# First two experts' remainders on VectorE instead of GpSimd, and the last token tile's modulation on VectorE behind its choice of experts

## The chip, the cores and the metric

The kernel runs on one core of a Trainium2 chip, as one launch. The metric is the device time of the launch in microseconds; the median of three runs of the kernel before is 1519.3 us.

## The reference

The reference is a two-layer block over 512 latent and 256 context tokens of 1024 features. Each layer computes a modulated norm, an input projection, three mixers (attention, a state space scan, a Hyena convolution), an output projection with a gated residual, a second modulated norm and a mixture of 16 experts, of which a router picks two for each token. The part that matters here:

```python
        xl = xl + gt1[:, None, :] * mix_l
        ...
        hl2 = modulate(rmsnorm(xl, g_ffn[i]), sh2, sc2)
        ...
            xl = xl + gt2[:, None, :] * grouped_moe(hl2, w_router, router_bias, w_gate[i], w_up[i], w_down[i])

def grouped_moe(h, w_router, router_bias, w_gate, w_up, w_down):
    scores = jax.nn.sigmoid((t @ w_router).astype(jnp.float32))
    ...
    for e in range(N_EXPERTS):
        y = (jax.nn.silu(t @ w_gate[e]) * (t @ w_up[e])) @ w_down[e]
        out = out + combine[:, e:e + 1] * y
```

The first layer routes all 768 tokens, the second only the 512 latent ones.

## The kernel before

**Precision.** A weight or activation that enters a matmul is split in two: a rounded copy (fp32r, made by ScalarE, L209) and the remainder, the difference between the value and its copy (a subtraction, L210). Three matmuls (L222 to L224: copy by copy, copy by remainder, remainder by copy) stand for one product. The subtraction runs on VectorE, or on GpSimd where the caller of `split_in` gives `lo_eng`.

**Output projection and routing** (`out_proj`, L971 to L1073). It goes over tiles of 128 tokens: six in layer 0, four in layer 1. `first(t)` multiplies and adds the gated residual, writes the new stream to DRAM (`xd`, by the queue of SyncE), takes the row norm and modulates: `h2 = x * rs * A2 + B2`, written to `hd` in DRAM, from which the experts gather their rows. For all tiles but the last, VectorE does the product (L1029) and GpSimd the sum (L1030). For the last tile ScalarE scales (L1026) and GpSimd does both the product with A2 (L1027) and the sum (L1030), each over 128 x 1024 numbers. `second(t)` makes the router's logits (its weights hold the modulation already, so it reads the unmodulated tile), and after the last tile of a group (0-1, 2-3 and 4-5 in layer 0; 0-2 and 3 in layer 1) `choose` (L1116) picks each token's two experts: about 40 small operations of VectorE, one behind the other, with a sigmoid of ScalarE at the head (kept as `R.scored`) and some small matmuls in between. Its end is the table of each expert's tokens (L1205, L1206). `order` and `places` (L1215, L1238) sort the experts; the cast at L1246 is kept as `mark`.

**Experts** (`experts`, L1478). An expert's weights come in six pieces of 512 KB by SyncE's queue into a ring of raw buffers (5 in layer 0, 8 in layer 1), are copied (L209) into a ring of 12 or 10, and their remainders follow (L210); a raw buffer is free again when both are done. Pieces 0 to 3 serve the first product, 4 and 5 the second. `NPE[l][n]` says how many of the six remainders of the n-th expert of a layer are made on GpSimd, for the first two experts: 3 and 3 in layer 0, 5 and 3 in layer 1. All later experts have 2 of 6 there. For each tile of an expert the rows are gathered from `hd` (L1374, a DMA that GpSimd issues), transposed by TensorE (L1389), copied (L1395) and their remainder made on VectorE (`xl`, L1396); the products follow, with the gated product at L1425 (`g`) and its copy and remainder (`gl`, L1445) between the two.

**What sets the order.** The tile framework's scheduler puts every engine's instructions in an order by a simulated timeline when the program is built; where several are ready in it, the earlier one of the program goes first, and an engine that would be idle there takes a later one. On the chip each engine then works in that fixed order. `tc.issue_after(ins)` queues a block's instructions of `ins`'s own engine behind `ins`. The first experts' splits stand under it: in layer 0 both behind `mark` (an instruction of VectorE), in layer 1 the first behind `R.scored` (of ScalarE) and the second behind `mark`. So the first expert's VectorE remainders in layer 1 are held back only by their copies, and GpSimd's are not held back by either.

```python
early = mark is not None and n < len(NPE[l])
gen = expert_weights(l, e, wp, NPE[l][n] if early else 2, ...)
...
with tc.issue_after((mark if n >= NI[l] else R.scored).ins) if early else ExitStack():
    w = list(gen) if early else [next(gen)]
```

Of the kernel before, what the change touches and what calls it, by code (L numbers as in the profile page):

```python
# [14 lines left out]
AF = mybir.ActivationFunctionType  # L15
# [16 lines left out]
# feature-major blocks of the input projection: 6 hyena, 5 ssd conv, 3 gate  # L32
# [6 lines left out]
# columns of the constant array  # L39
# [15 lines left out]
# columns of the per-feature vectors: c, c_ctx, then per layer  # L55
# [4 lines left out]
# rows that every partition holds  # L60
# [25 lines left out]
# places of the experts: the first or last few stay where they are, the others come in the order of their tokens;  # L86
# that many of the first places have a second tile
NS = (1, 3)
LAST = (False, True)
KD = (6, 2)  # L90
# rows of each place's first tile, and of the second
# [4 lines left out]
NPE = (3, 3), (5, 3)  # L96
# [9 lines left out]
# the most rows of a light expert  # L106
LIGHT = 64, 0
# tiles of tokens that choose their experts together: the first, how many
# [7 lines left out]
def limits(l):  # L116
    """above how many tokens a place's last tile is left to a further one"""
    big = 1e9
    return [(P + CAP2[l][q] if CAP2[l][q] < P else big) if q < KD[l] else CAP[l][q] if CAP[l][q] < P else big
            for q in range(NE)]  # L120
# [3 lines left out]
def most_further(l):  # L124
    """the most further tiles that any counts of tokens ask for; all places but the NS that stay in falling order"""
# [16 lines left out]
def tile_kernel(tc, I, out, dbg=None):  # L142
# [10 lines left out]
    def banks(cfg):  # L153
        """shares the banks out among the chains that run side by side: kinds, number of banks; 0: of the first two"""
        if rings.get("cfg") == cfg:
            return
        if "end" in rings:
            rings["end"]()
        g = tc.tile_pool(name="psum", bufs=1, space=bass.MemoryType.PSUM, reuse_waits="tile")
        rings.update(cfg=cfg, pool=g.__enter__(), end=lambda: g.__exit__(None, None, None))  # L160
# [51 lines left out]
    def split_in(pool, nm, n, src, raws, his, lo_eng=None, raw_pool=None, raw_tag=None, parts=None):  # L212
        """a load in two parts"""
# [13 lines left out]
    # zeros around the two columns: a window of 32 has them where a block wants its rows  # L227
# [8 lines left out]
    def adaln_end():  # L236
        """the sums over the four groups of rows that the blocks of features have, by features"""
# [7 lines left out]
    def adaln(l, ch, wp, mb, j, n, step, wp2=None):  # L245
        """a block of 128 features; n of them, step apart, share a bank; it is the j-th of these"""
# [65 lines left out]
    def filters(pool):  # L312
# [11 lines left out]
        for l in range(DEPTH):  # L324
# [18 lines left out]
            # sum and difference of the two directions  # L343
# [13 lines left out]
            for c in cs:  # L357
# [6 lines left out]
                for o in range(2):  # L364
                    SD = pool.tile([P, 4, 2, 256], F32, name="SD", bufs=2)
                    for i in range(2 * n):
# [9 lines left out]
                        if i == 0:  # L376
                            # lag 0: the second direction has none, the first takes the bias
# [35 lines left out]
    def to_features(l, v, xn, pool, hh, hl, ks=range(8)):  # L413
        """normalised rows of a group of tokens: modulated, by features, in two parts"""
# [16 lines left out]
    def norm1(pool, wp, hh, hl):  # L431
        """the first norm, each block of features as soon as its modulation is there"""
        xt = [pool.tile([P, D], F32, name=f"xt{t}") for t in range(TA)]
        ss = sm.tile([P, TA], F32, name="ss0", bufs=1)
        for t in range(TA):
            SP.dma_start(xt[t], I["xin"][t * P:(t + 1) * P])
            # the squares themselves are not needed: they go where the last features will be
# [47 lines left out]
    def hy_proj(l, wp, hh, hl, pool, u, filler):  # L485
        """v split by parity of the token, x1 likewise, x2 by features"""
# [316 lines left out]
    def kv_weights(l, wp, places, lo_eng=None):  # L803
        """places: of the two parts, where not in the ring"""
# [26 lines left out]
    def rotate(l, qr, pool):  # L831
        """norm and rotation of queries and keys, where they are"""
        rl = l * RL_N
        # rotary tables with the gains of the norm
# [50 lines left out]
    def to_heads(l, qr, pool, QT, KT):  # L885
        """queries and keys by features, in two parts"""
# [84 lines left out]
    def out_proj(l, wp, wr, mix, pool, choose):  # L971
# [8 lines left out]
        def gates(v):  # L980
# [4 lines left out]
            # the router behind the modulation: its weights take the scale, the shift becomes a row  # L985
# [21 lines left out]
        def first(t, mh, ml, xt):  # L1007
# [17 lines left out]
            if t == nt - 1:  # L1025
                ACT.activation(h2, xt, AF.Copy, scale=rs)  # L1026
                POOL.tensor_mul(h2, h2, A2)  # L1027
            else:
                DVE.scalar_tensor_tensor(h2, xt, rs, A2, OP.mult, OP.mult)  # L1029
            POOL.tensor_add(h2, h2, B2)  # L1030
            SP.dma_start(hd[s], h2)
            yield xt, rs
# [27 lines left out]
        for t in range(nt):  # L1060
# [8 lines left out]
            nxt = next(g)  # L1069
            if last is not None and t < nt - IL:  # L1070
                second(t - 1, *last)
            last = nxt
        second(nt - 1, *last)  # L1073

    class Route:
        """each token's two experts, their slots and weights; tokens and weights of each tile, the expert of each place"""

        def __init__(self, l, nt, pool):
            self.l, self.nt, self.pool, self.H, self.NS = l, nt, pool, nt, NS[l]
            # those that stay, and those that are sorted  # L1080
# [19 lines left out]
        def tile(self, m, sh, nm):  # L1100
            """for m tiles of tokens, with the place for the most of them"""
# [3 lines left out]
        def first_max(self, x, m, n, rev, op, out):  # L1105
            """one-hot of the first of the largest, or what is left of it"""
# [9 lines left out]
        def choose(self, t0, m, lg):  # L1116
            """for m tiles of tokens from the t0-th"""
# [24 lines left out]
            # place of the token among those of its expert  # L1142
# [10 lines left out]
            # token and weight  # L1153
# [25 lines left out]
            # token and weight of each expert's n-th token  # L1179
# [21 lines left out]
            else:  # L1201
                if t1 == nt:
                    # of those that stay
# [4 lines left out]
        def pick(self, dst, v, n):  # L1208
            """of each place, what its expert has"""
# [5 lines left out]
        def order(self):  # L1215
            pool, pos, b0, sr = self.pool, self.pos, self.b0, self.sr
            nr = NE - self.NS
            # those that stay keep theirs, the others come in the order of their counts
# [19 lines left out]
        def places(self):  # L1238
# [10 lines left out]
            # light experts have sets of features one below the other  # L1249
# [8 lines left out]
        def where(self, i):  # L1258
            """of a tile: the expert that stays, or none, and the column of the tile"""
# [19 lines left out]
        def slots(self):  # L1279
            """rows of each token's two experts, the experts of the further tiles and the number of those"""  # L1280
            pool, nt, K, pos = self.pool, self.nt, KD[self.l], self.pos
            self.nov = nov = most_further(self.l)
            # the experts with more tokens than the tiles of their places hold
# [30 lines left out]
            # slots: tile of the place, second tile of the place, further tile  # L1314
# [11 lines left out]
            # expert of further tile o: the number of experts whose further tiles end at or before o  # L1326
# [11 lines left out]
        def further(self):  # L1338
            """tokens and weights of the further tiles"""
            pool, H, nov = self.pool, self.H, self.nov  # L1340
            # the further tile that each 128 tokens of each expert have; those with a place have none
# [18 lines left out]
    def expert_weights(l, e, wp, n_pool, tag, bufs, light):  # L1360
        """in six parts, each when it is asked for"""
# [16 lines left out]
    def groups(c):  # L1378
        """a light expert's few tokens: their sets of features that lie side by side on the array"""
        return 4 if c == 32 else 2  # L1380
# [24 lines left out]
    def expert_up(st, k0, k1, pool):  # L1405
# [11 lines left out]
        if xl is None:  # L1417
            # the first half of the groups is the gate, the other what it acts on
# [9 lines left out]
    def expert_mid(st, g, pool):  # L1428
# [3 lines left out]
        if light and groups(c) == 4:  # L1432
            # both halves of the features at once
# [44 lines left out]
    def experts(l, jobs, R, gate, wp, pool, mark=None):  # L1478
        """jobs: the tiles of an expert with their rows, and the expert"""
# [29 lines left out]
    def combine(l, order, si, xt, gate, pool, hh=None, hl=None):  # L1509
        """gate: of the two groups of tokens, or the gain of the last norm second"""  # L1510
# [31 lines left out]
    def weave(*gens, stop=None):  # L1542
        """steps of each in turn, at its rate; what they yield, if anything"""
# [15 lines left out]
    for l in range(DEPTH):  # L1559
# [26 lines left out]
        if l == 0:  # L1586
            wp, close_wp = opened("win", 2, side="right")
            kp, close_kp = opened("kv", side="right")
            # the first half lies where the results of the attention will be
# [382 lines left out]
```

## Time and profile before

| | us |
|---|---|
| median of 3 runs | 1519.3 |
| lowest and highest | 1517.98, 1522.31 |
| span of the profiled execution, first to last instruction | 1512.0 |
| own time of the profiled execution | not given; the median stands 7.3 above its span |
| TensorE, VectorE, ScalarE, GpSimd busy | 1270.4, 957.4, 656.3, 563.7 |

Spans are read from the first instruction. The work around the change lies at 540 to 680 (layer 0) and 1220 to 1320 (layer 1); the experts' stages go on to about 853 and 1481. In a row of a timeline stand the start, the duration, the engine, the line of the code, the operation, what is written and read, and in brackets how long the engine was idle before it and what ended that. A "q" behind an engine's name is its queue.

### The profile page before, as it was taken

To read this page: it belongs to the slowest core of one execution; us is meant where nothing else is said; L and a number is where in the kernel's file an instruction comes from. 1 tells how busy PE (TensorE), PEld (TensorE's weight loads), DVE (VectorE), ACT (ScalarE), POOL (GpSimd) and SP (SyncE) were. 2 spreads that over 40 slices of the span, in tenths; PEclk is the share of its full clock that TensorE was granted. 3 is DMA by queue.
4 is the path that set the end of the run, shared out by engine and by line. 5 is a ranking of instruction groups with operands and counts; after the bars stand their busy time and mean duration, and the time that the engine had idled before them with its cause. 6 is when DMAs were issued, how large, how long until landed. Compare 5 with 4: busy or idle time off the path is not lost. (4 is left out here: it accounts for less than half of the span.)

```text
span 1512.0 us, 24116 instructions
## 1 busy us (share of the span) xinstructions
PE 1270.4 (84%) x8787; PEld 964.7 (64%) x8787; DVE 957.4 (63%) x1824; ACT 656.3 (43%) x1244; POOL 563.7 (37%) x496
## 2 busy tenths in 40 slices
PE   5999999899799799669999539989898892699991
PEld 3787877677577587547656228867676782576540
DVE  6754732734767865893544384844597748877974
ACT  5331324445333542333544363544545624366662
POOL 3120311444343523262323360410486244544653
PEclk9999999997899999769999859999998996699996
DMA  8745976345555252178999851111311453688984
GB/s 297 244 147 175 294 231 228 97 143 181 185 159 171 101 198 98 56 240 313 341 327 333 287 214 57 57 56 43 133 50 43 156 210 119 236 297 296 358 314 177
DMA packets 102775, 289.67 MB, mean 192 GB/s; under 512 B 11421, under 2 KB 24109, under 8 KB 102000
## 3 DMA queue, kind: packets, MB, share of 16 engines
q1 hardware_dynamic: 89632, 243.92, 47.1%
q0 software_dynamic: 8480, 30.81, 5.9%
q10 hardware_dynamic: 4528, 13.24, 2.4%
q8 instruction: 73, 1.20, 0.3%
q14 instruction: 62, 0.51, 0.1%
HBM read 241.98 MB, written 45.95 MB: 190 GB/s over the span
## 5 line engine op out<-in xcount | busy, mean ns | idle before, releaser
L209 ACT CAST he<-re 128x1024 fp32r<-128x1024 f32 x150 | 153.0, 1048 | 74.7 <-DMA re<-in_we_dram 27.8
L210 POOL TENSOR_TENSOR le<-re,he 128x1024 fp32r<-128x1024 f32 x56 | 141.3, 2538 | 97.3 <-ACT he L209 74.6
L222 PE MATMUL bank<-hh,hw 128*128 128x512 f32 (+1 forms) x440 | 160.5, 365 | 3.2 <-ACT hw L209 3.2
L223 PE MATMUL bank<-hl,hw 128*128 128x512 f32 (+1 forms) x440 | 157.9, 359 | 0.0
L224 PE MATMUL bank<-hh,lw 128*128 128x512 f32 (+1 forms) x440 | 156.3, 356 | 0.4 <-DVE lw L210 0.4
L210 DVE TENSOR_TENSOR le<-re,he 128x1024 fp32r<-128x1024 f32 x94 | 138.2, 1494 | 22.7 <-ACT he L209 22.7
L222 PE MATMUL bank<-he,xh 128*128 128x512 f32 (+3 forms) x264 | 107.7, 408 | 2.1 <-DVE g L1425 2.0
L224 PE MATMUL bank<-he,xl 128*128 128x512 f32 (+3 forms) x264 | 105.7, 402 | 2.6 <-DVE xl L1396 2.6
L223 PE MATMUL bank<-le,xh 128*128 128x512 f32 (+3 forms) x264 | 106.3, 403 | 0.8 <-DVE le L210 0.8
L933 POOL TENSOR_SCALAR pt<-pt,su 128x768 f32<-128x768 f32 (+1 forms) x60 | 55.8, 934 | 115.4 <-DVE su L932 112.0
L1374 POOL DMA_INDIRECT xg<-hd,tk x40 | 43.9, 1096 | 140.1 <-PE bank L1389 53.1
L222 PEld LDWEIGHTS bank<-hh,hw 128*128 128x128 f32 x440 | 85.7, 195 | 15.6 <-ACT hw L209 3.3
L223 PEld LDWEIGHTS bank<-hl,hw 128*128 128x128 f32 x440 | 85.6, 194 | 12.0 <-issue 1.2
L224 PEld LDWEIGHTS bank<-hh,lw 128*128 128x128 f32 x440 | 84.6, 192 | 12.4 <-DVE lw L210 0.9
L259 PE MATMUL bank<-mraw,c 128*32 128x128 f32 x1536 | 70.4, 295 | 15.7 <-DMA mraw<-in_wm_dram 11.8
L210 DVE TENSOR_TENSOR lw<-rw,hw 128x1024 fp32r<-128x1024 f32 x34 | 41.7, 1228 | 55.3 <-ACT hw L209 52.6
L948 PE MATMUL bank<-ph,vt 128*64 128x128 f32 x624 | 54.7, 296 | 16.7 <-DVE ph L945 7.3
L209 ACT CAST hw<-rw 128x1024 fp32r<-128x1024 f32 (+1 forms) x36 | 37.7, 1049 | 70.8 <-PE bank L223 39.8
L259 PEld LDWEIGHTS bank<-mraw,c 128*32 128x32 f32 x1536 | 40.0, 114 | 40.1 <-DMA mraw<-in_wm_dram 16.5
L223 PE MATMUL bank<-lo,mh 128*128 128x512 f32 x160 | 63.0, 395 | 0.8 <-DVE lo L210 0.8
L222 PE MATMUL bank<-ho,mh 128*128 128x512 f32 x160 | 63.5, 400 | 0.0
L926 DVE TENSOR_REDUCE mx<-banks 128x1 f32<-128x768 f32 (+1 forms) x60 | 50.2, 844 | 20.6 <-PE banks L923 20.5
(501 smaller groups left out, 3323.5 us busy)
## 6 DMA issues: line engine op xcount, KB each, us to landing
re<-in_we_dram SPq DMA_DIRECT2D x150, 512.0 KB, 5.9
mraw<-in_wm_dram SPq DMA_DIRECT2D x192, 256.0 KB, 3.6
we<-in_we_dram SPq DMA_DIRECT2D x42, 512.0 KB, 6.3
rw<-in_wi_dram SPq DMA_DIRECT2D x34, 512.0 KB, 3.6
ybuf<-zt SPq DMA_DIRECT2D x17, 512.0 KB, 7.3
ro<-in_wo_dram SPq DMA_DIRECT2D x16, 512.0 KB, 5.4
G<-ar SPq DMA_DIRECT2D x10, 768.0 KB, 4.0
ybuf<-y ACTq DMA_DIRECT2D x13, 512.0 KB, 8.0
```

Of the source, the lines that this page charges most:

```text
L209: ACT.copy(hi, src)
L210: (lo_eng or DVE).tensor_sub(lo, src, f(hi))
L222: PE.matmul(o, lh, rh, start=start, stop=False)
L223: PE.matmul(o, lh, rl, start=False, stop=False)
L224: PE.matmul(o, ll, rh, start=False, stop=stop)
L259: PE.matmul(ps[32 * k:32 * k + 32, 0:P], c32[:, 4 * h + k, 30 - 2 * j:62 - 2 * j], raw[:, k], start=(j + h == 0), stop=(j == n - 1 and h = ...
L926: DVE.tensor_reduce(mx, ps, axis=AX.XY, op=OP.max)
L933: POOL.tensor_scalar(pt[:, 0:nkt * P], pt[:, 0:nkt * P], su, 1.0, OP.mult, OP.mult)
L948: PE.matmul(po[64 * q:64 * q + 64, 0:P], vt[:, k0 + kt + j, h // 3], ph[:, (2 * j + q) * P:(2 * j + q + 1) * P], start=(kt + j == 0), stop ...
L1374: POOL.indirect_dma_start(out=xg[0:c], out_offset=None, in_=hd, in_offset=bass.IndirectOffsetOnAxis(ap=R.token(i)[0:c], axis=0))
```

## The change

The two entries of `NPE` become zeros, so that all twelve remainders of a layer's first two experts are made on VectorE. The modulation of a token tile becomes a step of its own in `first`. For all tiles but the last it is taken at the place it had. For the last tile it is taken at the very end of `out_proj`, behind `second(nt - 1)` and so behind the last `choose`; there VectorE does the product and the scaling in one operation (as in the other tiles) and the sum as well. ScalarE's scaling (L1026) is gone. The rest of the diff removes comments.

```diff
-NPE = (3, 3), (5, 3)
+NPE = (0, 0), (0, 0)
...
             SP.dma_start(xd[s], xt)
             rs = rstd_of(xt, h2)
-            if t == nt - 1:
-                ACT.activation(h2, xt, AF.Copy, scale=rs)
-                POOL.tensor_mul(h2, h2, A2)
-            else:
-                DVE.scalar_tensor_tensor(h2, xt, rs, A2, OP.mult, OP.mult)
-            POOL.tensor_add(h2, h2, B2)
+            yield xt, rs
+
+            e2 = DVE if t == nt - 1 else POOL
+            DVE.scalar_tensor_tensor(h2, xt, rs, A2, OP.mult, OP.mult)
+            e2.tensor_add(h2, h2, B2)
             SP.dma_start(hd[s], h2)
-            yield xt, rs
+            yield
...
             nxt = next(g)
+            if t < nt - 1:
+                next(g)
             if last is not None and t < nt - IL:
                 second(t - 1, *last)
             last = nxt
         second(nt - 1, *last)
+        next(g)
```

## Rows read from the trace of the kernel before

**Rows 1.** The page: span, engines' busy time, DMA issues of split expert pieces.
```profile
span 1512.0 us, 24116 instructions
...
PE 1270.4 (84%) x8787; PEld 964.7 (64%) x8787; DVE 957.4 (63%) x1824; ACT 656.3 (43%) x1244; POOL 563.7 (37%) x496
...
re<-in_we_dram SPq DMA_DIRECT2D x150, 512.0 KB, 5.9
```

**Rows 2.** Windows: length, busy PE, PEld, DVE, ACT, POOL, granted clock, DMA share, GB/s.
```profile
660.00:680.00 20.00, 14.20 (x61) 11.04 (x60) 17.96 (x34) 8.62 (x13) 10.81 (x5) 0.84 0.85 283
...
700.00:720.00 20.00, 20.00 (x169) 13.62 (x161) 6.46 (x11) 8.23 (x15) 4.76 (x4) 1.00 0.96 349
...
1260.00:1280.00 20.00, 0.93 (x9) 0.86 (x9) 19.79 (x53) 7.05 (x9) 12.23 (x7) 0.50 0.29 97
...
1400.00:1420.00 20.00, 20.00 (x100) 11.72 (x98) 16.71 (x23) 14.67 (x21) 12.07 (x6) 1.00 1.03 368
```

**Rows 3.** Timeline, layer 1, 1255 to 1273.5, all engines: the middle of the routing.
```profile
1255.66 2.34 POOL L1027 TENSOR_TENSOR h<-h,A 128x1024 f32<-128x1024 f32 x1 [11.73 <-ACT h L1026]
...
1255.93 2.09 DVE L1112 TENSOR_TENSOR eq<-eq,cst 128x12 f32<-128x12 f32 x1
...
1258.32 7.66 ACT L209 CAST he<-re 128x1024 fp32r<-128x1024 f32 x8
1260.38 11.67 POOL L210 TENSOR_TENSOR le<-re,he 128x1024 fp32r<-128x1024 f32 x5
...
1269.77 3.35 DVE L210 TENSOR_TENSOR le<-re,he 128x1024 fp32r<-128x1024 f32 x1
```

**Rows 4.** Timeline, layer 1, VectorE: such operations by themselves, and one idle wait.
```profile
1240.18 1.28 DVE L1029 SCALAR_TENSOR_TENSOR h<-ox,rs,A 128x1024 f32<-128x1024 f32 x1
...
1254.09 0.21 DVE L1123 TENSOR_TENSOR sel<-lg,row 128x48 f32<-128x48 f32 x1 [0.95 <-ACT lg L1121]
...
1279.69 0.17 DVE L1112 TENSOR_TENSOR eq<-eq,cst 128x16 f32<-128x16 f32 x1
...
1294.99 1.21 DVE L210 TENSOR_TENSOR le<-re,he 128x1024 fp32r<-128x1024 f32 x1
```

**Rows 5.** Timelines, layer 1, SyncE's and GpSimd's queues: last tile's write, first gather.
```profile
1273.58 0.38 SPq L1031 DMA_DIRECT2D hd<-h  x1
...
1287.89 1.06 POOL L1374 DMA_INDIRECT xg<-hd,tk  x1 [8.07 <-DVE tk L1205]
```

**Rows 6.** Timelines, layer 1, VectorE and TensorE behind the choice.
```profile
1290.02 4.80 DVE L210 TENSOR_TENSOR le<-re,he 128x1024 fp32r<-128x1024 f32 x2
...
1301.23 2.37 DVE L1304 TENSOR_TENSOR ob<-oi,ov 128x16 f32<-128x16 f32 x1
...
1303.86 2.30 DVE L1318 TENSOR_TENSOR v<-rk,v 128x8 f32<-128x8 f32 x1
...
1317.36 0.69 PE L1439 MATMUL bank<-cst,g 128*128 128x128 f32 x2 [7.02 <-DVE g L1425]
```

**Rows 7.** Timeline, layer 0, VectorE beside the last tile's modulation.
```profile
624.37 1.98 DVE L1054 SCALAR_TENSOR_TENSOR lg<-lg,rs,sh 128x16 f32<-128x16 f32 x1
...
626.46 2.30 DVE L1162 TENSOR_TENSOR tw<-wt,wsu 128x4 f32<-128x4 f32 x1
```

**Rows 8.** Timelines, layer 0, VectorE and TensorE at the first two experts.
```profile
646.88 5.22 DVE L210 TENSOR_TENSOR le<-re,he 128x1024 fp32r<-128x1024 f32 x1
...
655.67 2.20 DVE L1396 TENSOR_TENSOR xl<-bank,xh 128x512 fp32r<-128x512 f32 x4
...
659.64 2.36 DVE L1291 TENSOR_TENSOR lim<-cnt,lim 128x16 f32<-128x16 f32 x1
...
671.44 2.89 DVE L1334 CAST ei<-eo 128x13 int32<-128x13 f32 x1
...
656.40 0.80 PE L224 MATMUL bank<-he,xl 128*128 128x512 f32 x1 [2.60 <-DVE xl L1396]
...
675.81 0.58 PE L1439 MATMUL bank<-cst,g 96*128 96x96 f32 x2 [5.80 <-DVE g L1425]
```

## The prediction

> **What bounds the kernel now.** I read the page first: TensorE is busy for 1270 of 1512 us and no other engine for more than 957 [rows 1]. So a change to VectorE and GpSimd can only pay where TensorE stands still. The windows show two such places at the change. From 660 to 680 TensorE works 14.2 of 20 us, from 1260 to 1280 it works 0.9, its granted clock at 0.50, the lower level, while VectorE is busy for 19.8 [rows 2]. That looks like a saturated VectorE. The timeline of that stretch says otherwise: an operation over 12 numbers a row takes 2.09 us beside GpSimd's product over 1024 [rows 3], where the same line takes 0.17 later, beside an idle GpSimd [rows 4]. In the routing of layer 1 seven VectorE operations are drawn out in this way, the first at 1255.93 and the last, a remainder of 3.35 us, at 1269.77, while GpSimd works without a pause: two operations of the modulation, then five remainders in 11.67 us [rows 3]. All seven read two operands from SBUF, and each ends when a GpSimd operation does. So GpSimd's work does not run beside VectorE's here; VectorE waits for it, and the routing, on which the first gather depends, waits with it.
>
> **Layer 1, up to the table.** *Removed:* the seven take 16.65 us together, by the first and last of them [rows 3] 5.44 alone; by themselves they would take six times 0.17 to 0.19 and 1.21 [rows 4], 2.24 in all. That frees 14.4 us. *Added:* five more remainders on VectorE at 1.21 [rows 4], 6.05 us. They are not held behind `mark`, and the one that was there stands in the midst of the choice, about 1 us of copying behind the sigmoid, so I let all five stand on the path: bounds 0 (they fall into idle moments) and 6.05, and I take 6.05 because the one row there is shows it. *Modulation:* 1.28 for the product [rows 4] and some 1.21 for the sum, which no row shows on VectorE at this shape, so by the remainder of the same shape (bounds 0.7, an addition over half the row length, and 2.34, GpSimd's). It is ready when the row norm is, and the program puts it behind the choice, but the scheduler gives it to an idle VectorE: 0.95 us stand empty just then, ahead of the choice [rows 4]. So 2.49 less 0.95, 1.5 us on the path (bounds 0 and 2.5). ScalarE's scaling falls away, beside the path. Gain 14.4 - 6.05 - 1.5 = 6.8 us.
>
> The moved step also issues the write of `hd`. It left SyncE's queue at 1273.58, behind a load that waited for a raw buffer, and the first gather was issued at 1287.89 [rows 5], so 14 us of slack cover it; with the raw buffer free earlier it leaves earlier too. If the sum were put last of all, behind the choice, the write would end behind the table and the gather would wait for it, a few us; the scheduler would have to leave VectorE idle for that. Costed at nothing.
>
> **Layer 1, behind the table.** Two remainders took 4.80 us there with one of GpSimd's in between [rows 6]; the second expert's fourth remainder comes to VectorE in its place: 4.80 - 2.42 - 1.21 = 1.2 us, of which I count half, since TensorE has 16 transposes to do meanwhile: 0.6. At 1301 to 1306 the last two remainders of the second expert on GpSimd draw out two small operations to 2.37 and 2.30 [rows 6]; 4.3 us go, 2.42 come: 1.9, and it comes off the 7.02 us that TensorE then waits for `g` [rows 6]. Layer 1 in all: 9.3 us.
>
> **Layer 0.** Here both experts' VectorE remainders are held behind `mark`, so the choice meets only the modulation. It drew out two operations to 1.98 and 2.30 [rows 7], 3.9 us over the 0.2 that such small ones need [rows 4]; 2.49 come to VectorE, with hardly an idle moment: gain 1.4 (bounds 0 and 3.9). At the first expert a remainder takes 5.22 [rows 8], 4.0 too many, and two of GpSimd's come in front of `xl`, 2.42: gain 1.6, on the path, as TensorE waits for `xl` at 656.40 [rows 8]. Then four operations are drawn out, the first to 2.36 at 659.64 and the last to 2.89 at 671.44 [rows 8], 10.1 us in all and 9.3 over the 0.2 each that they need, against four remainders at 1.21, 4.8: VectorE reaches `g` 4.5 us sooner, and TensorE's wait of 5.80 for it [rows 8] shrinks by that. What is late next is the second expert's pieces, which land at the rate of the stream. Layer 0 in all: 1.4 + 1.6 + 4.5 = 7.5 us.
>
> **From there to the end.** Whether a head start lasts depends on what sets the pace of the experts. TensorE is busy for the whole of 700 to 720 and 1400 to 1420 [rows 2], so by the profile it is TensorE, and a head start lasts in full. But the DMA engines are at 0.96 and 1.03 of their time in the same windows [rows 2], so pieces may come late for a TensorE that is ahead. The stream too starts sooner, since the raw buffers are free sooner, and 48 MB at 349 GB/s are 137 us, less than either stage lasts. Between half and all, I take three quarters: 0.75 x (9.3 + 7.5) = 12.6 us. The profiled execution's span is 1512.0, and would be 1499.4. Its own whole time is not given; the median is 7.3 above the span, and I take that as unchanged: 1506.7, said as 1507.
>
> **A rule against it.** VectorE is busy for 19.8 of 20 us in the stretch [rows 2]. The Trainium skill, Perfetto Trace Analysis, Optimizing Scalar/DVE Operations, says that where VectorE is saturated it may make sense to hand work to ScalarE or even GpSimd, and this change does the reverse; the same section warns that GpSimd and VectorE share an SBUF read port, so that moving work between those two may not help. The drawn-out operations bear out the warning and not the advice.
>
> **Rivals.**
> 1. *VectorE's queue blocks on weights* (slower). VectorE works in order. A remainder of a piece that has not landed, put in front of an operation that TensorE waits for, stops both. In layer 0 only five raw buffers exist, so seven of the twelve remainders wait for pieces that come later. The first raw buffer comes free at 648.1 (646.88 and 1.21), its piece lands 5.9 us later [rows 1], six more follow at 1.85 each (512 KB at the 283 GB/s of that window [rows 2]), and the last is copied and subtracted in 2.2: 667.3. If all seven stand ahead of `xl`, that moves there from 655.67 [rows 8], 11.6 us later; the choice still gains 1.4, and layer 1 0.75 x 6.8. 1519.3 + 11.6 - 1.4 - 5.1 = 1524.4. Layer 0 loses from the first such piece ahead of `xl`, the whole from about four. For it: nothing but the order on VectorE holds these back. Against: in the order of before the small operations and `xl` come ahead of the later pieces' remainders. 8 in 100.
> 2. *No change: the routing pays what it saves.* VectorE's six remainders in layer 1 wait for ScalarE's copies, eight of which take 7.66 us [rows 3], and the modulation stands in front of the last choice in full: 14.4 - 6.05 - 2.5 - 2 of waiting = 3.9, nothing from layer 0, where remainders delay `g` as GpSimd's did: 1515.4. Against: the copies follow each other in 0.96 us, faster than VectorE's 1.21. 14 in 100.
> 3. *VectorE's busy time is work and not waiting.* Then 14 remainders at 1.21 and two modulations at 2.49 come on top, 22 us: 1541. The advice of the Trainium skill's page named above would give this. Against it stands 2.09 us against 0.17 for one line. 2 in 100.
> 4. *The move does little.* The scheduler takes VectorE's modulation early in either order, so "behind the choice" may not be what is seen. It is in the sum already and is worth at most 2.5 us a layer.
>
> **How the numbers follow.** A measurement of this kernel tells about 0.3%, 4.6 us, from no change. My forecast, a gain of 12.6, has 76 in 100 and lies beyond that. Rival 2 is within it, 14; rivals 1 and 3 are slower, 10. For the range: with the subtractions and modulation in idle moments the gains are 14.4 + 0.6 + 1.9 and 3.9 + 1.6 + 5.8, 28 us at a full carry, of which I leave out the end that needs all of it at once: 1496. With a carry of half, the modulations in full (8.3 in layer 1) and layer 0's `g` no sooner (3.0), (8.3 + 3.0) / 2 = 5.6 remain, 1514; the range goes to 1516 to take in rival 2.
>
> **What would show it.** In the changed profile no small operation of VectorE is above 1 us between the last sigmoid and the table, in either layer; L1027 is gone and GpSimd holds no remainder of the first two experts. The six remainders of layer 1's first expert stand inside the choice, at 1.2 us each. The first gather of layer 1 comes about 7 us sooner behind the last sigmoid's tile, TensorE's wait of 5.80 in layer 0 is near 1, that of 7.02 near 5. I am wrong if VectorE idles in front of remainders for copies or pieces, if TensorE gets idle places between 690 and 840 that it does not have, or if the waits at `g` stay as long.

## The result, and the profile after

The median is 1500.75 us (four executions, 1496.50 to 1507.02) against 1518.64 for the kernel before on the same chip (four, 1513.61 to 1522.31): a ratio of 0.9893, interval 0.9861 to 0.9924, so some 16 us faster. Medians and ratios go by executions in the fast state; one of run 7's ten (2098.29 us, granted clock 0.556) was not, and is left out. The forecast of 1507 (1496 to 1516) had the sign, the mechanism and most of the size; the time came out below it.

The page of the kernel after, span, busy times and the two groups of the experts' remainders:

```profile
span 1505.1 us, 24116 instructions
...
PE 1281.6 (85%) x8787; PEld 972.8 (65%) x8787; DVE 938.5 (62%) x1842; ACT 654.6 (43%) x1242; POOL 527.5 (35%) x478
...
L210 DVE TENSOR_TENSOR le<-re,he 128x1024 fp32r<-128x1024 f32 x108 | 145.5, 1370 | 35.0 <-ACT he L209 34.8
...
L210 POOL TENSOR_TENSOR le<-re,he 128x1024 fp32r<-128x1024 f32 x42 | 106.9, 2556 | 101.6 <-ACT he L209 89.5
```

VectorE got 14 remainders and two modulations more and is busy for 18.9 us less than before [rows 1]: what left it was waiting that the profile counts as busy.

The two profiles differ by 6.9 us only, since each stands at an edge of its kernel's executions: 1513.61 is the fastest of the four of before, 1507.02 the slowest of the four of after. So the comparison goes by stretches between marks that every trace has. The marks are, in both layers, the row norm of the last token tile (L410), the table of tokens (its copy to `tk`) and the last expert matmul (L224). Timelines of the kernel before, VectorE and TensorE:

```profile
622.41 0.16 DVE L410 RECIPROCAL rs<-rs 128x1 f32<-128x1 f32 x1 [0.54 <-ACT rs L409]
...
643.23 0.16 DVE L1205 TENSOR_TENSOR tk<-tab,bank 128x2 int32<-128x2 f32 x1 [1.72 <-PE bank L1196]
...
852.96 0.40 PE L224 MATMUL bank<-he,gl 128*96 128x512 f32 x1
...
1252.99 0.15 DVE L410 RECIPROCAL rs<-rs 128x1 f32<-128x1 f32 x1
...
1287.44 0.16 DVE L1205 TENSOR_TENSOR tk<-tab,bank 128x6 int32<-128x6 f32 x1 [1.29 <-PE bank L1196]
...
1480.61 0.40 PE L224 MATMUL bank<-he,gl 128*32 128x512 f32 x1
```

The same marks in every kernel of this study (starts of L410 and `tk`, end of L224), in us. "Mixers" is the stretch of layer 1 that lies between the two stages, which no edit here touches:

| kernel | layer 0: norm to table | norm to last expert | mixers | layer 1: norm to table | norm to last expert | both stages |
|---|---|---|---|---|---|---|
| before | 20.82 | 230.95 | 399.63 | 34.45 | 228.02 | 459.0 |
| before, second profile | 20.80 | 229.98 | 405.09 | 34.66 | 228.38 | 458.4 |
| after | 18.68 | 223.16 | 406.78 | 26.95 | 220.36 | 443.5 |
| modulation alone | 18.69 | 228.61 | 410.86 | 31.71 | 225.33 | 453.9 |
| modulation alone, second profile | 18.69 | 229.42 | 414.58 | 31.38 | 226.77 | 456.2 |
| remainders alone | 20.80 | 224.88 | 403.11 | 28.95 | 221.18 | 446.1 |
| GpSimd subtractions put back, unread | 18.69 | 222.91 | 405.84 | 34.74 | 226.31 | 449.2 |
| GpSimd zeros, unread | 18.69 | 221.79 | 405.59 | 26.96 | 219.21 | 441.0 |
| modulation held behind the choice | 18.60 | 222.57 | 405.66 | 25.19 | 216.74 | 439.3 |
| all later remainders on VectorE | 18.68 | 228.54 | 413.83 | 26.84 | 211.87 | 440.4 |
| first experts held behind the table | 18.68 | 222.78 | 410.43 | 20.41 | 215.61 | 438.4 |
| combined | 18.15 | 224.02 | 406.51 | 24.92 | 208.44 | 432.5 |
| combined, first experts held | 18.60 | 223.89 | 408.99 | 18.88 | 204.24 | 428.1 |

In the two kernels with the first experts held, the mark itself has moved: layer 1's last norm comes 4.5 us later behind the one before it than in all the others, so their last three columns look better, and their mixers worse, than they are (run 8).

The two stages win 7.8 and 7.7 us, 15.5 together, close to the 16 that the ratio gives. The profiles hide 7.2 of it in the mixers. TensorE's idle time there is the same in both (399.63 - 327.04 = 72.6 and 406.78 - 333.93 = 72.9 us); the 7.2 lie in its busy time, at a granted clock of 0.91 in the one profile and 0.89 in the other. The second profile of the unchanged kernel has 0.89 as well, and mixers of 405.09. So this is the executions' spread (the rows are with run 11).

Where the 7.5 us of layer 1's routing came from: timelines of the kernel after, layer 1, VectorE first, then SyncE's queue, GpSimd and TensorE:

```profile
1255.57 1.28 DVE L1028 SCALAR_TENSOR_TENSOR h<-ox,rs,A 128x1024 f32<-128x1024 f32 x1
...
1257.26 1.22 DVE L1029 TENSOR_TENSOR h<-h,B 128x1024 f32<-128x1024 f32 x1
...
1259.13 0.17 DVE L1114 TENSOR_TENSOR eq<-eq,cst 128x12 f32<-128x12 f32 x1
...
1260.23 1.23 DVE L210 TENSOR_TENSOR le<-re,he 128x1024 fp32r<-128x1024 f32 x1
...
1263.07 2.35 DVE L210 TENSOR_TENSOR le<-re,he 128x1024 fp32r<-128x1024 f32 x2
...
1281.29 0.16 DVE L1207 TENSOR_TENSOR tk<-tab,bank 128x6 int32<-128x6 f32 x1 [0.55 <-PE bank L1198]
...
1297.41 1.23 DVE L210 TENSOR_TENSOR le<-re,he 128x1024 fp32r<-128x1024 f32 x1 [2.51 <-ACT he L209]
...
1306.97 2.27 DVE L1320 TENSOR_TENSOR v<-rk,v 128x8 f32<-128x8 f32 x1
...
1258.50 0.32 SPq L1030 DMA_DIRECT2D hd<-h  x1
...
1282.24 1.08 POOL L1376 DMA_INDIRECT xg<-hd,tk  x1 [7.99 <-DVE tab L1208]
...
1305.70 3.53 POOL L210 TENSOR_TENSOR le<-re,he 128x1024 fp32r<-128x1024 f32 x1 [11.36 <-ACT he L209]
...
1307.16 0.50 PE L222 MATMUL bank<-he,gh 128*128 128x512 f32 x1 [0.68 <-ACT gh L1443]
...
1309.72 0.69 PE L1441 MATMUL bank<-cst,g 128*128 128x128 f32 x2 [1.36 <-DVE g L1427]
```

The operation over 12 numbers that took 2.09 us takes 0.17 [rows 3], the six remainders take 1.2 each inside the choice, and TensorE's wait of 7.02 [rows 6] has become 0.68 and 1.36. Where GpSimd still has a remainder (the third expert's, at 1305.70), a small operation of VectorE is still drawn out, to 2.27. And the modulation stands ahead of the choice: the scheduler took it as soon as the norm was there, whatever the program's order.

The same in layer 0:

```profile
627.58 0.23 DVE L1053 SCALAR_TENSOR_TENSOR lg<-lg,rs,sh 128x16 f32<-128x16 f32 x1
...
646.72 1.22 DVE L210 TENSOR_TENSOR le<-re,he 128x1024 fp32r<-128x1024 f32 x1
...
661.16 0.17 DVE L1293 TENSOR_TENSOR lim<-cnt,lim 128x16 f32<-128x16 f32 x1
...
666.21 1.23 DVE L210 TENSOR_TENSOR le<-re,he 128x1024 fp32r<-128x1024 f32 x1 [3.65 <-ACT he L209]
...
654.52 0.50 PE L224 MATMUL bank<-he,xl 128*128 128x512 f32 x1 [0.66 <-DVE xl L1398]
...
668.38 0.69 PE L1441 MATMUL bank<-cst,g 128*128 128x128 f32 x2 [3.47 <-DVE g L1427]
```

1.98 has become 0.23 [rows 7], 5.22 has become 1.22 and 2.36 has become 0.17 [rows 8]. TensorE's wait for `xl` fell from 2.60 to 0.66, the longest one for `g` from 5.80 to 3.47 [rows 8].

### The profile page after: what moved, and what is told of

It is laid out like the page before. It is cut to its first block, busy times and chain, and to the rows that moved or that the text cites. A ratio compares the mean times of both kernels' runs of the same rounds, so it can differ in the third digit from the quotient of the medians.

```text
span 1505.1 us, 24116 instructions
## 1 busy us (share of the span) xinstructions
PE 1281.6 (85%) x8787; PEld 972.8 (65%) x8787; DVE 938.5 (62%) x1842; ACT 654.6 (43%) x1242; POOL 527.5 (35%) x478
## 5 line engine op out<-in xcount | busy, mean ns | idle before, releaser
L210 DVE TENSOR_TENSOR le<-re,he 128x1024 fp32r<-128x1024 f32 x108 | 145.5, 1370 | 35.0 <-ACT he L209 34.8
L224 PE MATMUL bank<-hh,lw 128*128 128x512 f32 (+1 forms) x440 | 157.0, 358 | 0.4 <-DVE lw L210 0.4
L210 POOL TENSOR_TENSOR le<-re,he 128x1024 fp32r<-128x1024 f32 x42 | 106.9, 2556 | 101.6 <-ACT he L209 89.5
L224 PE MATMUL bank<-he,xl 128*128 128x512 f32 (+3 forms) x264 | 104.7, 398 | 0.7 <-DVE xl L1398 0.7
L224 PEld LDWEIGHTS bank<-hh,lw 128*128 128x128 f32 x440 | 85.4, 194 | 12.6 <-DVE lw L210 0.9
L209 ACT CAST hw<-rw 128x1024 fp32r<-128x1024 f32 (+1 forms) x36 | 37.7, 1048 | 73.5 <-PE bank L223 38.2
L948 PE MATMUL bank<-ph,vt 128*64 128x128 f32 x624 | 55.4, 298 | 16.1 <-DVE ph L945 7.4
L224 PE MATMUL bank<-ho,ml 128*128 128x512 f32 x160 | 63.1, 394 | 0.0
```

The lines of the kernel that those rows point to most:

```text
L209: ACT.copy(hi, src)
L210: (lo_eng or DVE).tensor_sub(lo, src, f(hi))
L224: PE.matmul(o, ll, rh, start=False, stop=stop)
L948: PE.matmul(po[64 * q:64 * q + 64, 0:P], vt[:, k0 + kt + j, h // 3], ph[:, (2 * j + q) * P:(2 * j + q + 1) * P], start=(kt + j == 0), stop ...
```

## The experiments

Theory A: a GpSimd operation that reads two operands from SBUF stops a VectorE operation that reads two, so each one on GpSimd costs VectorE its own length wherever VectorE has something to do. Rivals: that any work of GpSimd does it, that the gain came from the modulation or the order and not from the remainders, and, for the later runs, that a saving in the routing is owed again at the experts. Every kernel here computes the whole reference; two do unread work besides, as said there. Diffs are against the kernel after; the letters of an expectation's theories are its own.

**1. The modulation alone.**

```diff
-NPE = (0, 0), (0, 0)
+NPE = (3, 3), (5, 3)
```

> The modulation moved, the remainders as before (3, 3 and 5, 3 on GpSimd). Theory A (GpSimd's operations with two operands stop VectorE's): only the modulation's two stops go, 3.9 us less 2.5 of new VectorE work in layer 0 and about as much in layer 1, so the interval from the last tile's row norm to the experts' end shrinks by 1 to 3 us in each layer; whole kernel 2 to 5 us faster than before, ratio about 0.998. Theory B (the gain comes from remainders that are ready sooner and raw buffers that are free sooner, not from the stops): nearly nothing, ratio 1.000. Theory C (the moved modulation is the main part of the gain): ratio 0.991 or less.

Measured: 1524.26 (twelve executions) against 1517.26, ratio 1.005 (1.0026 to 1.0074): slower, by half a per cent. The stages are nevertheless 2.3 and 2.7 us shorter. The loss lies in the mixers, 410.86, which begin 210 us behind layer 0's table and end ahead of layer 1's routing. Run 11 takes that up.

**2. The remainders alone.** The modulation as in the kernel before:

```diff
+            if t == nt - 1:
+                ACT.activation(h2, xt, AF.Copy, scale=rs)
+                POOL.tensor_mul(h2, h2, A2)
...
-            e2.tensor_add(h2, h2, B2)
+            POOL.tensor_add(h2, h2, B2)
```

> All twelve remainders of the first two experts on VectorE, the modulation as before (ScalarE, then GpSimd twice). Theories A and B: most of the gain, 11 to 14 of the 16 us, ratio about 0.991. Under A GpSimd's two modulation operations still draw out VectorE operations to about 2 us, two in layer 0 and two in layer 1, and the table of layer 1 comes 1 to 3 us later behind the last row norm than in the changed kernel (26.9 us there). Theory C: ratio 0.998.

Measured: 1503.73 (six), ratio 0.991 (0.9877 to 0.9942). The remainders carry the gain: 12.9 of 15.5 us in the stages. Layer 1's table is 2.0 us later than in the kernel after. Timelines of this kernel, GpSimd and VectorE, layer 1:

```profile
1251.41 2.34 POOL L1027 TENSOR_TENSOR h<-h,A 128x1024 f32<-128x1024 f32 x1 [11.73 <-ACT h L1026]
...
1251.83 1.94 DVE L1112 TENSOR_TENSOR eq<-eq,cst 128x12 f32<-128x12 f32 x1
...
1253.83 2.35 POOL L1030 TENSOR_TENSOR h<-h,B 128x1024 f32<-128x1024 f32 x1
...
1254.03 2.17 DVE L1114 TENSOR_TENSOR og<-cst,mx 128x12 f32<-128x12 f32 x1
```

Two GpSimd operations, two stops of 1.94 and 2.17, each ending with its GpSimd operation. The two parts sum to 5.0 + 12.9 = 17.9, against 15.5 for both together; with run 1's second profile (456.2) they sum to 15.7, so that difference is within the spread.

**3. The cause put back without the work.** Five subtractions of a piece from itself on GpSimd, beside layer 1's first expert, into a tile that nobody reads. VectorE's own work, and the order on every engine otherwise, are those of the kernel after:

```diff
+                if dup and j:
+                    POOL.tensor_sub(dup[0], f(hi), f(hi))
```

> The changed kernel, in which GpSimd makes five more subtractions of 128 x 1024 in layer 1 at the place where it had the first expert's remainders; nothing reads their results, and no weight is copied, subtracted or freed later for them. Theory A: VectorE is stopped about five times 2.1 us between the sigmoid and the table, table 26.9 + 10 = 37 us behind the last row norm, kernel 8 to 10 us slower than the changed one. Theory B: table stays at 26.9 us, time as the changed kernel's.

Measured: 1510.14 (ten), ratio 0.9951 (0.993 to 0.9973); the table of layer 1 7.8 us later, at 34.74, where the kernel before has it. Timelines, GpSimd and VectorE:

```profile
1258.51 12.74 POOL L1374 TENSOR_TENSOR dup<-he 128x1024 fp32r<-128x1024 f32 x5 [15.94 <-ACT he L209]
...
1258.66 1.90 DVE L1113 TENSOR_TENSOR eq<-sm,mx 128x48 f32<-128x48 f32 x1
...
1260.64 1.86 DVE L1130 TENSOR_TENSOR pr<-sel 128x4 f32<-128x4 f32 x1
...
1263.56 1.89 DVE L1114 TENSOR_TENSOR eq<-eq,cst 128x48 f32<-128x48 f32 x1
...
1265.46 4.04 DVE L210 TENSOR_TENSOR le<-re,he 128x1024 fp32r<-128x1024 f32 x2
...
1269.60 3.87 DVE L210 TENSOR_TENSOR le<-re,he 128x1024 fp32r<-128x1024 f32 x2
```

Work that nothing depends on delays the routing by 7.8 us: the stop is shown, and no dependence on the remainders' results is needed for it. I had expected 10. The five take 12.74 and not 5 x 2.35, so GpSimd waited for VectorE as well. The five drawn-out rows are 1.5 to 1.7 us longer each than the same rows of the kernel after, 8.3 together, so a GpSimd operation cost VectorE less than its own length here, though VectorE was not idle in that stretch.

**4. GpSimd busy without reading.** Ten times zeros over the same 1024 columns in that place, and one column copied on ScalarE that starts them; all unread:

```diff
+                    POOL.memset(f(dup[0]), 0.0)
+                    POOL.memset(f(dup[0]), 0.0)
```

> The changed kernel, in which GpSimd fills the same unread tile with zeros ten times at that place (128 x 1024 each, so it is busy about as long but reads nothing from SBUF), behind one added ScalarE copy of a column. Theory A with the stop due to the reading of SBUF: VectorE is not stopped, table at 26.9 to 27.5 us behind the last row norm. If any busy GpSimd stops VectorE: about 35 us.

Measured: one execution, 1501.73; layer 1's table at 26.96, as without them (26.95). Timelines, GpSimd and VectorE:

```profile
1267.58 0.95 POOL L1377 MEMSET dup<- 128x1024 f32 x1
...
1267.60 1.02 DVE L1191 TENSOR_TENSOR os<-cst,ix 128x512 f32<-128x512 f32 x2
```

VectorE's pair of 512 columns takes 1.02 beside a memset, and no longer than beside an idle GpSimd. So a busy GpSimd does not stop VectorE, a reading one does. The zeros ran beside the second half of the choice (from 1262.54), not the first, so only that half tests it; and no run has a GpSimd operation that reads one operand.

**5. The kernel before, a second profile.** No edit.

> The kernel before once more, for a second profile of it. If layer 1's mixers (from the end of layer 0's experts to the last row norm of layer 1, 399.6 us in the first profile, 406.8 in the changed kernel, 410.9 with the modulation alone) differ because another order of instructions came out of the scheduler there, they take 398 to 401 us again; if it is chance from run to run, up to 407. The two routing stages take 231 and 228 us again.

Measured: 1518.59, span 1516.3. The stretches stand in the table: the stages agree within 1 us with the first profile's, the mixers are 5.5 us longer, 4.5 of them in TensorE's busy time. That is the spread against which the other rows are to be read; the two profiles of run 1's kernel differ by 2.3 in the two stages together.

**6. The modulation really behind the choice.** Its two operations are made to wait for the last choice's sum of one-hots:

```diff
-        next(g)
+        with tc.issue_after(choose.__self__.chosen.ins):
+            next(g)
...
-            DVE.tensor_add(self.oh[:, t0:t1], o[:, :, 0], o[:, :, 1])
+            self.chosen = DVE.tensor_add(self.oh[:, t0:t1], o[:, :, 0], o[:, :, 1])
```

> The changed kernel, with the last tile's modulation queued behind the last choice's one-hot sum on VectorE, so that it really stands behind the choice. If the modulation cost the path 1.5 us a layer as forecast, the table of layer 1 comes 0.5 to 2.5 us sooner behind the row norm than 26.9 us (VectorE waits there for TensorE for 1.9 us in all, which the modulation can fill), layer 0's as much sooner than 18.7; kernel 1 to 4 us faster than the changed one. Rival: the write to DRAM comes so late that the first gather waits for it, and the gather's rows land 1 to 3 us later behind the table than 6.2 us: no gain.

Measured: 1497.51 (four), ratio 0.9865 (0.9823 to 0.9907); layer 1's table 1.8 us sooner, layer 0's 0.1. Timelines, VectorE and SyncE's queue, layer 1:

```profile
1269.22 1.28 DVE L1028 SCALAR_TENSOR_TENSOR h<-ox,rs,A 128x1024 f32<-128x1024 f32 x1
...
1270.54 1.23 DVE L1029 TENSOR_TENSOR h<-h,B 128x1024 f32<-128x1024 f32 x1
...
1271.79 0.33 SPq L1030 DMA_DIRECT2D hd<-h  x1
```

VectorE does them while it would wait for TensorE's products for the choice of the tiles before (2.90 us from 1268.10). The write of `hd` leaves 21.3 us behind the norm (1250.54 in this trace), in the kernel after 4.2, and from the table to TensorE's first transposes of the gathered rows it is 5.6 us, no longer than before (5.9): no gather waits for it. The prediction's 1.5 us for the modulation on the path is about the 1.8 that this frees.

**7. All later experts' remainders on VectorE too**, in both layers:

```diff
-NPE[l][n] if early else 2, *("re"
+NPE[l][n] if early else 0, *("re"
```

> The changed kernel, with the remainders of all the experts on VectorE (the later ones have two of six on GpSimd). If GpSimd's subtractions stop VectorE everywhere, VectorE gets freer in the experts' stages as well, and the small idle places of TensorE there (under 5 us in each layer) go: 1 to 5 us faster than the changed kernel, since TensorE is the bound there. Rival: VectorE becomes the bound in layer 1 (28 more subtractions of 1.21 us, 34 us, and no stops to save where it was waiting anyway): 3 to 10 us slower.

Measured: 1510.04 (nine), ratio 0.9954 (0.992 to 0.9988), by the ratio worse than the kernel after, with intervals that just touch. But by stages: layer 1 8.5 us shorter, layer 0 5.4 longer, mixers 413.83, in which TensorE is idle for 80.0 (run 11). Windows of this kernel (length, busy TensorE, weight loads, VectorE, ScalarE, GpSimd, granted clock, DMA share, GB/s), one in either layer's experts:

```profile
690.00:850.00 160.00, 150.49 (x864) 93.23 (x862) 78.46 (x111) 65.72 (x112) 14.23 (x15) 0.98 0.87 315
...
1320.00:1460.00 140.00, 139.51 (x680) 87.67 (x679) 129.17 (x176) 95.31 (x136) 16.79 (x13) 1.00 0.97 347
```

In layer 1 TensorE has hardly a gap left at a VectorE of 92%. In layer 0 it stands idle for 9.5 of 160, though VectorE is busy for half of it. Four waits of 4.1 us together, the longest of 1.85 at 708.26, end with ScalarE's copy of a gated product; what the rest comes from, no run settles. So whether the move pays is a matter of the stage, not of the kernel.

**8. Layer 1's first expert held behind the table**, as the others are:

```diff
-NI = (0, 1)
+NI = (0, 0)
```

> The changed kernel, with the first expert's remainders of layer 1 held behind the mark as well, so that none of them stands in the choice. If the six cost the path 6 to 7 us there, the table comes 6 to 7 us sooner behind the row norm than 26.9 us; then the ten remainders stand between the table and the first product, where VectorE has about 5 us to spare while the first gather is under way: first product 3 to 6 us later behind the table. In sum 0 to 3 us faster. Rival: the six fell into moments in which the choice waited anyway: table less than 3 us sooner, kernel slower by 2 to 5 us.

Measured: 1502.42 (four), ratio 0.9905 (0.9872 to 0.9939). Behind the last norm layer 1's table comes 6.5 us sooner, the end of its experts 4.7. But that norm itself comes 4.5 us later. Timelines of this kernel, VectorE, ScalarE and TensorE:

```profile
1236.47 0.16 DVE L410 RECIPROCAL rs<-rs 128x1 f32<-128x1 f32 x1 [2.32 <-ACT rs L409]
...
1254.03 0.16 DVE L410 RECIPROCAL rs<-rs 128x1 f32<-128x1 f32 x1 [0.34 <-ACT rs L409]
...
1245.41 6.73 ACT L209 CAST he<-re 128x1024 fp32r<-128x1024 f32 x7 [8.04 <-PE bank L223]
...
1252.67 0.66 PE L1043 MATMUL bank<-xT,wa 128*32 128x128 f32 x8 [5.26 <-ACT xT L1040]
```

From the last norm but one to the last it is 17.56 us here, 13.06 in the kernel after (1241.28 to 1254.34). `mark` is an instruction of VectorE, so it holds back the remainders but no longer ScalarE's copies, which `R.scored` had held: seven of them now stand ahead of the copy of `xT` for which TensorE waits, and the norm with it. Counted from the last norm but one, the table comes 2.0 us sooner (37.97 against 40.01), and the end of the experts at 233.17 against 233.42, which is nothing. So this run does not measure what the six remainders cost on the path: the edit moved the copies as well.

**9 and 10. Combined.** Run 6 with the later experts' remainders on VectorE in layer 1 alone; and the same with `NI = (0, 0)`:

```diff
-NPE[l][n] if early else 2, *("re"
+NPE[l][n] if early else (2, 0)[l], *("re"
```

> Theory A (a GpSimd remainder costs VectorE its own length wherever VectorE has work; in layer 1 VectorE has room for all remainders, in layer 0 it has not): modulation behind the choice keeps layer 1's table at 25.2 us behind the last tile's norm, and the later experts' remainders on VectorE in layer 1 take the stage from 216.7 to about 208 to 212 us; layer 0's stage stays at 222 to 223. The two stages together 430 to 434 against 459 before; time 0.979 to 0.985 of before. Theory B (the 8.5 us that layer 1 won with all remainders on VectorE came from that kernel's other order of the mixers ahead of it, not from the remainders): layer 1's stage stays at 215 to 218 and the time at 0.987.

> Adds to the run beside it that layer 1's first experts are also held back behind the table. Theory A: table 5 to 6 us sooner, about 19 to 20 us behind the norm; the remainders' six times 1.2 us then come between the table and the second product, so 2 to 4 us of it are given back; the time is 0.5 to 3 us below the run beside it, 0.977 to 0.984 of before. Theory B (the remainders are owed anyway and the stage is paced by the stream): same time as the run beside it, within 2 us.

Measured: 1493.27 (six), ratio 0.9834 (0.9805 to 0.9863), and 1491.43 (five), 0.9829 (0.9809 to 0.9848): some 25 us under the kernel before, both. The two times are not told apart. Stages 432.5 and 428.1; but the second's lead of 4.4 us comes from the mark that run 8 moved. From the last norm but one layer 1's table comes after 37.98 and 36.45 us, the end of the experts after 221.50 and 221.81: no lead. The page of the first of them:

```profile
L210 DVE TENSOR_TENSOR le<-re,he 128x1024 fp32r<-128x1024 f32 x136 | 162.3, 1217 | 31.7 <-ACT he L209 30.4
```

The mean of VectorE's remainders is 1217 ns, where it was 1370 in the kernel after: 28 more of them, 16.8 us more. In layer 1 alone, then, the later remainders won 216.74 - 208.44 = 8.3 us, and the mixers, at 406.51, had no share in it.

**11. The modulation alone, a second profile.**

> The same instructions as mod_only, a second profile. If that kernel's loss comes from the order that the scheduler gives layer 1's mixers, their interval is again 408 to 413 us, against 400 to 405 for the kernel before; if it was chance, it is at 400 to 406 this time. The stages again at 18.7 us (layer 0, to the table) and 31.7 us (layer 1, to the table).

Measured: 1528.61; the stages to the table at 18.69 and 31.38, the mixers at 414.58: 410.9 and 414.6 against 399.6 and 405.1. Windows over the mixers (length, busy TensorE, weight loads, VectorE, ScalarE, GpSimd, granted clock, DMA share, GB/s) of the kernel before, its second profile, the kernel after, and the modulation alone, twice:

```profile
853.36:1252.99 399.63, 327.04 (x2062) 266.46 (x2062) 252.37 (x444) 185.36 (x375) 159.00 (x158) 0.91 0.31 109
...
851.74:1256.83 405.09, 331.55 (x2062) 270.40 (x2062) 251.90 (x444) 185.32 (x375) 159.96 (x158) 0.89 0.30 108
...
847.56:1254.34 406.78, 333.93 (x2062) 272.06 (x2062) 250.56 (x443) 185.77 (x375) 160.68 (x158) 0.89 0.30 107
...
847.52:1258.38 410.86, 329.06 (x2062) 268.68 (x2062) 254.48 (x443) 190.52 (x379) 161.40 (x158) 0.90 0.30 106
...
853.93:1268.51 414.58, 333.44 (x2062) 272.99 (x2062) 254.63 (x444) 190.60 (x379) 161.14 (x158) 0.88 0.30 105
```

TensorE's busy time varies from execution to execution of one kernel, with the granted clock. Its idle time does not: 72.6 and 73.5 us in the kernel before, 72.9 in the kernel after, but 81.8 and 81.1 with the modulation alone. So some 8 us of idle time belong to that kernel. TensorE has the same instructions there in another order: compared one by one, 1002 of the 2062 stand in the same place as in the kernel before, in the kernel after 1892. The transposes of the queries, for one, begin 110.6 and 110.8 us behind the end of layer 0's experts, in the kernel before 115.7 and 115.8, and still the last products of the attention (L948) start later, after 352.4 and 356.3 us against 340.4 and 345.9. The scheduler has made another order of a part that nobody edited. That the idle time goes with the kernel is shown by two profiles of each; that the order is its cause is argued, since a kernel with the order of before and this modulation was not made.

## Why the prediction was right, and where it was off

The working by its own steps, predicted against measured, all from the last tile's norm. "Behind `g`" is a point at which TensorE has done the same work in both kernels, just behind the waits for `g` that the prediction names: the start of its 163rd instruction behind the norm in layer 0 and of its 159th in layer 1. (The start of the transposes of `g` themselves [rows 6, 8] is no such point: in the kernel after four products stand ahead of them that stood behind them before.)

| step | predicted gain | measured |
|---|---|---|
| layer 1, to the table: 14.4 - 6.05 - 1.5 | 6.8 | 7.5 |
| layer 1, behind `g` | 9.3 | 73.55 to 64.80: 8.8 |
| layer 0, to the table | 1.4 | 2.1 |
| layer 0, behind `g` | 7.5 | 62.29 to 52.68: 9.6 |
| both, at the end of the experts | 0.75 x 16.8 = 12.6 | 7.8 + 7.7 = 15.5 |

- **Mechanism: right.** Drawn-out operations are stops by GpSimd's reads; run 3 puts the cost back alone, run 4 shows that a busy GpSimd that reads nothing costs none. Two readings were too neat. The seventh drawn-out row does not end with GpSimd's last operation but 1.07 behind it (1273.12 against 1272.05 [rows 3]): it waited and then ran. And "two operands" is not the whole condition: the cast of 2.89 us [rows 8] reads one. GpSimd in the kernel before, and the same cast in the kernel after:

```profile
671.94 2.35 POOL L210 TENSOR_TENSOR le<-re,he 128x1024 fp32r<-128x1024 f32 x1
...
674.18 0.16 DVE L1336 CAST ei<-eo 128x13 int32<-128x13 f32 x1
```
- **Layer 1's sum: right.** The charge for the modulation (1.5) measured 1.8 in run 6. The five added remainders stand inside the choice; no run measures their 6.05 alone, but in run 2 the removal of five stops (14.4 less 3.9 for the two of the modulation) gained 5.5 at the table, which leaves 5.0 for them. The first gather, counted from the norm, left 7.0 us sooner (34.90 to 27.90), as foretold. Of the 7.5 at the table 5.0 reach the first expert's products, since TensorE now also waits 1.67 for the second gather's rows (at 1291.16); at `g` it is 8.8 again.
- **Layer 0's sum: 2.1 too small.** At `xl` 3.0 were forecast and 3.9 measured. For the clock nothing was forecast: the ten products behind TensorE's wait for `xl` take 4.43 us at a granted clock of 0.50, the lower level, in the kernel before, where TensorE had just stood idle for 2.60, and 2.43 at 1.00 in the kernel after, where it had for 0.66; that is 2.0. At `g` 4.5 were forecast and 3.7 measured. I wrote that the wait of 5.80 would be near 1. That wait, in front of the first expert's second tile, is gone, but TensorE now waits 3.47 for the first tile's `g`: VectorE stood idle for 3.65 in front of a remainder whose piece had not landed, and ScalarE, too, waited 5.15 for that piece ahead of its copy and did its half of `g` behind it. It is the beginning of rival 1, without its price: `xl` was not behind the late pieces.
- **The carry: a term that was mis-sized, a little.** "Between half and all, I take three quarters" rested on DMA engines at 0.96 and 1.03 [rows 2]. Of 18.4 us behind `g`, 15.5 were there at the end, 0.84. The doubt of a full carry was right: in layer 0 the head start falls from 9.6 to 6.5 between TensorE's 401st and 421st instruction behind the norm and is 7.8 at the end. The kernel after, TensorE:

```profile
714.20 0.50 PE L222 MATMUL bank<-he,gh 128*128 128x512 f32 x1 [1.68 <-ACT gh L1443]
```

  ScalarE had waited 4.96 us for a piece at 706.01, and two copies of weights (1.99 us at 711.88) stood right ahead of its copy `gh`. The granted clock is 0.87 from 709 to 722. Of the 2.9 us between 12.6 and 15.5, the head starts (18.4 for 16.8) make 1.2 and the carry 1.7.
- **The base.** I put the median 7.3 above the span and kept that. The profiled execution's own time was 1513.61, 1.6 above its span; the other 5.7 were its distance below the median, and as an offset for medians the 7.3 was fit.
- **The rivals.** 1: two idle waits of 3.65 and 2.51 on VectorE, and 1.7 us of gaps on TensorE from 690 to 840 (148.32 of 150 us busy, where it had all). Both are signs of being wrong that I had named; they came small, and no loss came of them in sum. 2: the routing did not pay what it saved; it gained 7.5 and 2.1. 3: fell, VectorE's busy time dropped by 18.9 us with more work on it; the advice of the Trainium skill, Perfetto Trace Analysis, Optimizing Scalar/DVE Operations, that it may make sense to hand work from a saturated VectorE to GpSimd, does not apply here, since VectorE was not saturated, and its warning of the shared port is borne out (2.09 against 0.17 us for one line [rows 3, 4]). 4: half right: "behind the choice" is not what the kernel does, and it costs 1.8 us in layer 1.
- **What I did not see:** that the remainders alone would be 0.9 % and the modulation alone a loss, through a stage that neither part edits.

## What to carry to other kernels

Where an engine's small operations have long and uneven durations, compare one line's duration beside a busy and an idle neighbour before calling the engine saturated: here moving work onto the "busier" engine shortened it, and moving all of layer 1's was worth another 8 us. Ask it per stage, since the same move lost in layer 0. And compare kernels by marks in the trace, not by spans: a scheduler that reorders a far stage can hide or invent some 10 us. Look at the marks, too: in run 8 the mark had moved by 4.5 us, and a gain of 6.5 behind it was one of 2.0. Here TensorE's idle time in the unedited stage told a kernel with another order (81 to 82 us against 73) from the spread of executions, which was in its busy time.

## What the runs showed of the hardware that was not expected

- The stop is mutual: beside VectorE's remainders five GpSimd subtractions took 12.74 us (run 3), 2.55 each on the mean, where single ones take 2.34 and 2.35 (run 2).
- Writing alone stops nothing: memsets of 0.95 us beside a pair of VectorE operations of 1.02, the same as without them (run 4).
- VectorE at 129 of 140 us (run 7, layer 1) and TensorE at 139.51: a VectorE of 92% did not bound the stage.
